# Half of the softmax transposes moved from TensorE to VectorE and a trip through DRAM, with the source's order on every engine

## The chip, the cores and the metric

The kernel runs on one core of a Trainium2 chip. What counts is the time on the device for one execution, in microseconds (us); every time below is in us unless ns is written. Three executions of the kernel before took 957.3, 958.48 and 962.88; the median is 958.48. A further execution was recorded by the hardware profiler, and all rows shown come from it.

## The reference, cut to what matters

One layer of an encoder block, for 512 tokens of width 2048. The normalised input is multiplied by one wide matrix whose columns feed two mixers, attention with 16 heads of 64 and a gated linear attention (GLA) with 4 heads; both results are gated and go through an output matrix.

```python
h = rms_norm(x) * (1.0 + scale[:, None]) + shift[:, None]
proj = h @ w_in[layer]
aq, ak, av, ag, gq, gk, gv, gg, lr_f, lr_b = jnp.split(proj, PROJ_SPLITS, axis=-1)
...
s = jnp.einsum('bnqrhe,bnkrhe->bhrnqk', qb, kw) * (E ** -0.5)   # one of three patterns
s = jnp.where(mask, s + bias[None, :, None, None], NEG_INF)
m = jnp.max(s, axis=-1, keepdims=True)
p = jnp.exp(s - m)
den = jnp.sum(p, axis=-1, keepdims=True)
o = jnp.einsum('bhrnqk,bnkrhe->bhrnqe', (p / den), vw)
...
a_out = att.reshape(B, S, ATT_WIDTH) * jax.nn.silu(ag)
g_out = g_o * jax.nn.silu(gg)
y = jnp.concatenate([a_out, g_out], axis=-1) @ w_out[layer]
return rms_norm(x + gate[:, None] * y) * final_gain
```

The three patterns are merged with weights from their softmax denominators. That is the same as one dense softmax over all 512 keys, with the logarithm of the number of patterns that hold a key added to the bias, and this is what the kernel computes. For each head it needs P, 512 by 512 after the softmax, once with queries on the partitions (for the sums over keys) and once turned, with keys on the partitions (for the product with the values).

## The kernel before, in words

**Units.** The big products are cut into units of 512 output columns: qk2, qk4, qk6 (queries and keys of two pairs of heads each), gk, gv0, gv1 (GLA's keys and values), ag0, ag1, gg0, gg1 (the gates), o0 to o3 (the output matrix). Two earlier stages, sa and sb, make the values and the first queries and keys. A unit has four output tiles, each in a PSUM buffer of its own, `ps_..._0` to `ps_..._3`, and 16 steps along the inner dimension of 2048, two to a fetched weight group. Every product is made of three TensorE matmuls (function `three`, L168 to L171), since numbers are split in a high part and a low rest: high by high, high by low, low by high.

**Weights.** A group of 512 KB is fetched on SyncE's queue (`fetch`, L282 to L286) into one of four RAW buffers, its high part is copied on ScalarE (`split_hi`, L313, 128x1024) and its low part taken by a subtraction on VectorE (`split_lo`, L297, 128x1024), into three buffers each.

**Attention as side work.** While TensorE goes through qk2, qk4, qk6 and gk, the four heads of the two pairs whose queries and keys the unit before made are attended to between its matmuls. A head has four tiles of 128 queries, so each unit has 16. The short names in the prediction are s, p and t with head and tile: s71 is the score of head 7's tile 1, p71 its P, t71 its turned tile. Each tile takes

- `score`: two matmuls (L576, L577) into a PSUM buffer of the "pa" tag (three of them), a pass on VectorE that adds the bias and takes the row's minimum of the negated logits (L580), exp on ScalarE (L583), a reciprocal on VectorE (L584) and a scaling on GpSimd (L585);
- `turn`: four TensorE transposes into a "pa" buffer (L597), a copy of the high part on ScalarE (L601) and the low rest on VectorE (L602), into `pt`, which holds two tiles (a half head);
- `values`, once a half: eight matmuls (L611), a copy on ScalarE (L614) and a sum on VectorE (L618) into `cat`.

A list `items` puts a tile's turn two places after its score and a half's products one after its second turn; `ATT_AT` spreads the list over the unit, and `unit` (L843) issues each item at its tick, 64 ticks to a unit.

**Between units** `qk_evict` (L531) empties the four output tiles: for each head ScalarE makes `qs` and `ks` (L539, L548), VectorE the rest of `qs` and `kl` (L540, L550), and four small transfers on SyncE's queue bring the other half of the partitions (L549, L551). Queries and keys lie in "pj" buffers, of which there are five, so the next unit's second tile needs the first of them emptied.

**Other side work.** The adaLN shift and gate need column sums over matrices that are read once: 48 sums on VectorE, `bias_half` for the values' bias (`rawv`) and `gate_half` (`rawg`, L244), each with a load of 512 KB on SyncE's queue. `SUMS_IN` says how many lie in each unit. The GLA heads lie beside gv1, ag0, ag1 and gg0.

**What sets the order.** TensorE always follows the order in which the source calls its instructions (`tc.manual_schedule(engines={E.PE})`). Up to the end of sb all engines follow a plan made in the kernel. From qk2 on the other engines, GpSimd, VectorE, ScalarE and SyncE (`PLANNED`), get their order from a scheduler that goes by priorities; side work is lifted by

```python
with tc.high_priority(offset=20):
    go()
```

Of the kernel before, what the change touches and what calls it, by code (L numbers as in the profile page):

```python
# [10 lines left out]
F32 = mybir.dt.float32  # L11
F32R = mybir.dt.float32r
# [60 lines left out]
ATT_AT = (0.17, 0.8, 0.04, 0.05, 0.05)  # L73
# [4 lines left out]
SUMS_IN = {"qk6": 4, "gk": 4, "gv0": 9, "gv1": 2, "ag0": 7, "ag1": 9, "gg0": 9}  # L78
# [55 lines left out]
def block_kernel(ctx: ExitStack, tc: tile.TileContext, a: dict):  # L134
# [147 lines left out]
    def fetch(i):  # L282
        if i < len(groups) and i not in raws:
            u, g = groups[i]
            raws[i] = RAW(f"raw_{u}{g}", [2, 512])
            nc.sync.dma_start(raws[i], a["w_" + u][g])  # L286
# [244 lines left out]
    def qk_evict(p, psq, psk):  # L531
# [3 lines left out]
        for j in range(2):  # L535
            own = slice(64 * j, 64 * j + 64)
            oth = slice(64 - 64 * j, 128 - 64 * j)
            qs = T2(f"qs{p}{j}", F32R)
            act(qs[own], psq[own, ::-1], AF.Copy, scale=-0.125)  # L539
            stt(qs[oth], psq[own, ::-1], -0.125, qs[own].bitcast(F32),  # L540
                op0=ALU.mult, op1=ALU.subtract)
            stacks[2 * p + j] = [qs, None, None, own]
        for j in range(2):
            own = slice(64 * j, 64 * j + 64)
            oth = slice(64 - 64 * j, 128 - 64 * j)
            ks = T2(f"ks{p}{j}", F32R)
            kl = T2(f"kl{p}{j}", F32R)
            act(ks[own], psk[own], AF.Copy)  # L548
            nc.sync.dma_start(ks[oth].bitcast(F32), ks[own].bitcast(F32))  # L549
            tt(kl[own], psk[own], ks[own].bitcast(F32), op=ALU.subtract)  # L550
            nc.sync.dma_start(kl[oth].bitcast(F32), kl[own].bitcast(F32))  # L551
            stacks[2 * p + j][1:3] = ks, kl
# [3 lines left out]
    def attention(pairs):  # L556

        tiles = [(2 * p + j, i) for p in pairs for j in range(2) for i in range(4)]
        gt, pt, pr_ = {}, {}, {}
        heads = [2 * p + j for p in pairs for j in range(2)]  # L560

        def g_load(h):
            g = gp.tile([P, 896], F32, tag="g", name=f"g{h}")
            nc.sync.dma_start(g, bass.AP(grow.tensor, grow.offset + h * 1024, [[1, P], [1, 896]]))
            gt[h] = g

        def score(h, i):
            def go():
                if h % 8 == 0 and i == 0:
                    cat[h // 8] = B8(f"cat{h // 8}", [4, 512])  # L570
# [12 lines left out]
                act(t, t, AF.Exp, bias=st[:, 0:1], scale=-1.0, accum_out=st[:, 1:2])  # L583
                nc.vector.reciprocal(st[:, 2:3], st[:, 1:2])  # L584
# [4 lines left out]
        def turn(h, i):  # L589
            def go():  # L590
# [7 lines left out]
                hi = pt[h, half][:, 0, :, P * ii:P * ii + P]  # L598
                lo = pt[h, half][:, 1, :, P * ii:P * ii + P]
# [4 lines left out]

        def values(h, half):
            def go():
                t = pt.pop((h, half))
# [24 lines left out]
        at = [start + (q + 0.5) / len(items) * span for q in range(len(items))]  # L632
        at[0] -= move0
        at[1] -= move1
        at[-1] += move_last
        return list(zip(at, items))
# [206 lines left out]
    def unit(name, natural, side=(), rhs=None, lr=None, tiles=range(4)):  # L843
# [5 lines left out]
        for q in range(KT // 2):  # L849
            g = gorder[q] if name == "o3" else q  # L850
            i0 = gi[name, g]
            todo = []
            if 0 in tiles:
                todo = list(range(gi[name, gorder[0] if name == "o3" else 0], upto[name, g] + 1))
                for i in todo:
                    split_hi(i)
                for ahead in (1, 2):
                    fetch(upto[name, g] + ahead)
            if i0 not in low:
                split_lo(i0)  # L860
            hi, lo = wts[i0]
            for n, i in enumerate(tiles):
                for kk in range(2):
# [267 lines left out]
```

## Time and profile before

| what | value |
|---|---|
| median of three executions | 958.48 |
| the profiled execution, whole | 959.9 |
| its span, first to last instruction | 957.9 |
| TensorE busy (page, share of the span) | 939.7 (98%) |
| VectorE busy | 605.3 (63%) |
| ScalarE busy | 431.5 (45%) |
| GpSimd busy | 81.1 (8%) |
| mean granted clock of TensorE | 0.997 |
| DMA, mean over the span | 171 GB/s |

The page counts an engine as busy while one of its instructions runs; the loads of weights into TensorE (PEld) overlap its matmuls and are counted apart. A busy share is a mean over stages. The views that follow break it down: stretches of the span, the time that an engine waited and for whom, and a timeline in which each instruction has its start, its length and, in brackets, the idle time before it and what ended that. A line number such as L597 is the line of the kernel that issued the instruction.

### The profile page before, as it was taken

What the parts mean: (1) busy time and instruction counts of PE and PEld (TensorE: products, weight loads), DVE (VectorE), ACT (ScalarE), POOL (GpSimd) and SP (SyncE); (2) the same over time, 40 slices, a digit from 0 to 9 for tenths busy, and PEclk for the clock granted to TensorE, in tenths of its full rate; (3) what the DMA queues carried; (4) which work ended last, traced back from release to release, by engine and by line L of the source; (5) the groups of instructions that cost most, each with busy time, mean ns of one, the idle gap of its engine ahead of it and who ended that gap; (6) DMA issues with size and microseconds to landing.
All of it is one profiled execution on the core that took longest, in us unless ns stands there. A gap on an engine that the chain in (4) does not pass through costs nothing.

```text
span 957.9 us, 11999 instructions
## 1 busy us (share of the span) xinstructions
PE 939.7 (98%) x4464; PEld 777.1 (81%) x4464; DVE 605.3 (63%) x900; ACT 431.5 (45%) x719; POOL 81.1 (8%) x100
## 2 busy tenths in 40 slices
PE   8999999999999999999999999999999999999996
PEld 5888788888888888888778888888887888888884
DVE  7988899675756676766435656675964352546421
ACT  5443533565655655655215544543834152233222
POOL 0000000012122022122000000000010000202120
PEclk9999999999999999999999999999999999999998
DMA  9999687443333463533454244354555464244013
GB/s 330 413 411 365 229 296 275 150 131 105 112 103 105 144 200 108 173 127 103 150 176 146 86 132 154 132 176 154 173 195 183 132 221 154 92 151 152 23 55 121
DMA packets 45180, 163.76 MB, mean 171 GB/s; under 512 B 5730, under 2 KB 6018, under 8 KB 40386
## 3 DMA queue, kind: packets, MB, share of 16 engines
q1 hardware_dynamic: 44946, 162.68, 49.9%
q8 instruction: 35, 0.57, 0.2%
q10 hardware_dynamic: 176, 0.33, 0.1%
q14 instruction: 23, 0.18, 0.1%
HBM read 154.51 MB, written 4.28 MB: 166 GB/s over the span
## 4 chain that ended last, share of the span: by engine, by line
PE 84%; DMA 6%; DVE 5%; issue 3%; ACT 1%; SPq 0%; POOL 0%; ACTq 0%; DVEq 0%; POOLq 0%
PE ps_o L170 6%; PE ps_o L169 6%; PE ps_o L171 6%; DMA rawg<-in_wg 6%; PE ps_qk L170 5%; PE ps_qk L169 5%; PE ps_qk L171 5%; PE o L611 3%; PE sta L169 3%; PE sta L170 3%; PE sta L171 3%; PE stb L171 3%; PE stb L169 3%; PE stb L170 3%; PE ps_gv L171 3%; PE ps_gv L170 3%
## 5 line engine op out<-in xcount | busy, mean ns | idle before, releaser
L585 POOL TENSOR_SCALAR p<-p,st 128x512 f32<-128x512 f32 x64 | 45.5, 711 | 406.6 <-DVE st L584 357.9
L244 DVE CUSTOM_DVE_ANT_0 cb<-cb,sb,c_bcond 128x2048 f32<-128x2048 f32 (+1 forms) x32 | 73.4, 2294 | 0.0
L583 ACT ACTIVATE p<-p,st 128x512 f32<-128x512 f32 x64 | 46.1, 721 | 56.8 <-DVE st L580 56.3
L602 DVE TENSOR_TENSOR pt<-t,pt 128x512 fp32r<-128x512 f32 x64 | 44.0, 689 | 16.2 <-ACT pt L601 15.8
L580 DVE CUSTOM_DVE_ANT_0 p<-s,g 128x512 f32<-128x512 f32 x64 | 43.6, 687 | 14.8 <-PE s L577 14.5
L601 ACT ACTIVATE pt<-t 128x512 fp32r<-128x512 f32 x64 | 37.8, 592 | 10.2 <-PE t L597 9.2
L244 DVE CUSTOM_DVE_ANT_0 rawg<-rawg,sb,gate 128x1024 f32<-128x1024 f32 x16 | 20.5, 1283 | 29.6 <-DMA rawg<-in_wg 29.6
L611 PEld LDWEIGHTS o<-pt,vv 128*128 128x128 f32 x256 | 34.7, 188 | 5.0 <-DVE pt L602 2.2
L597 PEld LDWEIGHTS t<-c_ident,p 128*128 128x128 f32 x256 | 31.8, 140 | 8.5
L597 PE MATMUL t<-c_ident,p 128*128 128x128 f32 x256 | 38.3, 272 | 0.0
L611 PE MATMUL o<-pt,vv 128*128 128x256 f32 x256 | 36.6, 283 | 0.9 <-DVE pt L602 0.8
L244 DVE CUSTOM_DVE_ANT_0 rawg<-rawg,sb,c_bcond 128x1024 f32<-128x1024 f32 x16 | 20.5, 1283 | 26.3 <-DMA rawg<-in_wg 26.3
L1014 POOL TENSOR_TENSOR x<-x,fgain 128x512 f32<-128x512 f32 x12 | 20.3, 1696 | 185.3 <-ACT ysq L1012 185.3
L1012 ACT ACTIVATE ysq<-x 128x512 f32<-128x512 f32 x16 | 10.1, 632 | 47.2 <-DVE x L1010 47.2
L767 POOL TENSOR_SCALAR dc<-st,sc 128x256 f32<-128x256 f32 x16 | 10.4, 652 | 245.5 <-DVE st L764 240.6
L1009 DVE TENSOR_TENSOR y<-ps_o,sb 128x512 f32<-128x512 f32 x16 | 10.9, 684 | 25.9 <-PE ps_o L171 25.9
L584 DVE RECIPROCAL st<-st 128x1 f32<-128x1 f32 x64 | 10.3, 162 | 24.9 <-ACT p L583 24.9
L576 PE MATMUL s<-ks,qs 128*128 128x512 f32 x64 | 25.1, 391 | 0.0
L577 PE MATMUL s<-kl,qs 128*128 128x512 f32 x64 | 25.0, 391 | 0.0
L774 ACT ACTIVATE sq<-st,sc 128x256 f32<-128x256 f32 x24 | 12.2, 509 | 26.8 <-DVE st L769 14.3
L1010 DVE TENSOR_TENSOR x<-y,x 128x512 f32<-128x512 f32 x16 | 18.0, 1125 | 0.3
L614 ACT ACTIVATE oh<-o 64x256 f32<-64x256 f32 x32 | 12.2, 382 | 13.0 <-PE o L611 12.2
(1275 smaller groups left out, 2916.7 us busy)
## 6 DMA issues: line engine op xcount, KB each, us to landing
cb<-in_wm SPq DMA_DIRECT2D x31, 1024.0 KB, 7.9
rawg<-in_wg SPq DMA_DIRECT2D x32, 512.0 KB, 3.4
raw_o<-in_w_o SPq DMA_DIRECT2D x32, 512.0 KB, 3.4
raw_qk<-in_w_qk SPq DMA_DIRECT2D x24, 512.0 KB, 3.4
rawb<-in_w_sb SPq DMA_DIRECT2D x16, 512.0 KB, 4.8
rawv<-in_wv SPq DMA_DIRECT2D x16, 512.0 KB, 3.8
raw_gv<-in_w_gv SPq DMA_DIRECT2D x16, 512.0 KB, 3.5
raw_ag<-in_w_ag SPq DMA_DIRECT2D x16, 512.0 KB, 3.3
```

The source lines that it names most:

```text
L169: mm(ps, lh, rh, start=first, stop=False)
L170: mm(ps, ll, rh, start=False, stop=False)
L171: mm(ps, lh, rl, start=False, stop=last)
L244: nc.vector.tensor_tensor_reduce(out=w, in0=w, in1=with_, op0=ALU.mult, op1=ALU.add, scale=1.0, scalar=init, accum_out=dst)
L576: mm(ps, qs[:, q], ks, start=True, stop=False)
L580: nc.vector.tensor_tensor_reduce(out=t, in0=ps, in1=gt[h][:, P * i:P * i + 512], op0=ALU.add, op1=ALU.min, scale=1.0, scalar=3e38, accum_o ...
L583: act(t, t, AF.Exp, bias=st[:, 0:1], scale=-1.0, accum_out=st[:, 1:2])
L585: nc.gpsimd.tensor_scalar(t, t, st[:, 2:3], 1.0, op0=ALU.mult, op1=ALU.mult)
L597: nc.tensor.transpose(pk[:, kt * P:kt * P + P], t[:, kt * P:kt * P + P], ident)
L601: act(hi, src, AF.Copy)
L602: tt(lo, src, hi.bitcast(F32), op=ALU.subtract)
L611: mm(po[:, :256], vv[h // 4][:, kt, h % 4, :], t[:, w, kt, :], start=kt == 0 and w == 0, stop=kt == 3 and w == 1)
```

## The change

P is turned in two ways now. In each of the four units, a tile whose head and half are listed in `BY_DVE` (both halves of the first head, the first half of the second and of the third: eight tiles of 16) is transposed by VectorE, which turns blocks of 32x32 in place; the result is stored to DRAM (`leave`, 256 KB) and a half's two tiles are loaded again in four transfers that put the blocks where they belong (`back`, 128 KB each, into a RAW buffer `pf`). ScalarE then makes the high part and VectorE the low rest of the whole half in one instruction each (`part_hi`, `part_lo`), and the products of this half stand later (`BACK_AT`). The other eight tiles go through TensorE as before (`pe_turn`). The reciprocal and the scaling are an item of their own (`scale`).

The order changes with it. From the start of qk2 to the end of gv0 all engines follow the source's order. In qk4, qk6 and gk the first two weight groups are gone through together, tile by tile, so that the second output tile is begun at the 5th step and not at the 3rd. The weights of qk and gk from the fourth group on, and the bias rows `g`, are fetched on ScalarE's queue. `SUMS_IN` takes eight column sums out of qk6 and gk; they stand in later units. The small `lr` weights are loaded and split within gk, and not after it.

```diff
-ATT_AT = (0.17, 0.8, 0.04, 0.05, 0.05)
+ATT_AT = (0.13, 0.0565)
+BY_DVE = ((0, 0), (0, 1), (1, 0), (2, 0))
+BACK_AT = (2.7, 4.6, 5.0, 6.6)
...
-SUMS_IN = {"qk6": 4, "gk": 4, "gv0": 9, "gv1": 2, "ag0": 7, "ag1": 9, "gg0": 9}
+SUMS_IN = {"gv0": 13, "gv1": 3, "ag0": 8, "ag1": 9, "gg0": 9}
...
-            nc.sync.dma_start(raws[i], a["w_" + u][g])
+            queue = nc.scalar if u[:2] in ("qk", "gk") and i > 2 else nc.sync
+            queue.dma_start(raws[i], a["w_" + u][g])
...
@@ qk_evict
-            qs = T2(f"qs{p}{j}", F32R)
+            qs, ks, kl = [T2(f"{n}{p}{j}", F32R) for n in ("qs", "ks", "kl")]
             act(qs[own], psq[own, ::-1], AF.Copy, scale=-0.125)
+            act(ks[own], psk[own], AF.Copy)
             stt(qs[oth], psq[own, ::-1], -0.125, qs[own].bitcast(F32),
                 op0=ALU.mult, op1=ALU.subtract)
-            stacks[2 * p + j] = [qs, None, None, own]
-        for j in range(2):
...
             tt(kl[own], psk[own], ks[own].bitcast(F32), op=ALU.subtract)
-            nc.sync.dma_start(kl[oth].bitcast(F32), kl[own].bitcast(F32))
-            stacks[2 * p + j][1:3] = ks, kl
+            for t in (ks, kl):
+                nc.sync.dma_start(t[oth].bitcast(F32), t[own].bitcast(F32))
+            stacks[2 * p + j] = [qs, ks, kl, own]
...
@@ attention
-            nc.sync.dma_start(g, bass.AP(grow.tensor, grow.offset + h * 1024, [[1, P], [1, 896]]))
+            nc.scalar.dma_start(g, bass.AP(grow.tensor, grow.offset + h * 1024, [[1, P], [1, 896]]))
...
+        def scale(h, i):
+            def go():
+                t, st = pr_.pop((h, i))
                 nc.vector.reciprocal(st[:, 2:3], st[:, 1:2])
                 nc.gpsimd.tensor_scalar(t, t, st[:, 2:3], 1.0, op0=ALU.mult, op1=ALU.mult)
                 pr_[h, i] = t
...
-        def turn(h, i):
+        def pe_turn(h, i):
...
+        def turn(h, i):
+            def go():
+                t = T2(f"pt{h}{i}")
+                nc.vector.transpose(t.rearrange("p (b k r) -> p k b r", b=4, k=4), pr_.pop((h, i)))
+                pr_[h, i] = t
+        def leave(h, i):
+            def go():
+                half, ii = divmod(i, 2)
+                if ii == 0:
+                    away[h, half] = dp.tile([2, P, 512], F32, tag=f"away{h}{half}", name=f"away{h}{half}")
+                nc.sync.dma_start(away[h, half][ii], pr_.pop((h, i)))
+        def back(h, half):
+            def go():
+                t = away.pop((h, half))
+                f = RAW(f"pf{h}{half}", [8, 128])
+                for b in range(4):
+                    nc.sync.dma_start(f[32 * b:32 * b + 32], bass.AP(
+                        t.tensor, t.offset + P * b, [[512, 32], [32 * 512, 8], [1, P]]))
+                pf[h, half] = f
+        def part_hi(h, half):
+            def go():
+                t = pt[h, half] = B8(f"pt{h}{half}", [2, 4, 256], F32R)
+                src = pf[h, half].rearrange("p b (k r) -> p k b r", k=4)
+                act(t[:, 0].rearrange("p k (b r) -> p k b r", b=8), src, AF.Copy)
+        def part_lo(h, half):
+            def go():
+                src = pf.pop((h, half)).rearrange("p b (k r) -> p k b r", k=4)
+                hi, lo = [pt[h, half][:, e].rearrange("p k (b r) -> p k b r", b=8) for e in range(2)]
+                tt(lo, src, hi.bitcast(F32), op=ALU.subtract)
...
-        for x in range(n + 4):
-            if x < n:
-                items.append(score(*tiles[x]))
-            if 2 <= x <= n + 1:
-                items.append(turn(*tiles[x - 2]))
-            if 3 <= x <= n + 2 and tiles[x - 3][1] % 2 == 1:
-                items.append(values(tiles[x - 3][0], tiles[x - 3][1] // 2))
+        for x in range(n):
+            h, i = tiles[x]
+            items.append((x, score(h, i)))
+            items.append((min(x + 0.75, n - 0.6), scale(h, i)))
+            half, ii = divmod(i, 2)
+            if (x // 4, half) in BY_DVE:
+                items.append((x + 1.1, turn(h, i)))
+                items.append((x + 1.5, leave(h, i)))
+                if ii:
+                    for at, piece in zip(BACK_AT, (back, part_hi, part_lo, values)):
+                        items.append((x + at, piece(h, half)))
+            else:
+                items.append((x + 1.8, pe_turn(h, i)))
+                if ii:
+                    items.append((x + 3.6, values(h, half)))
+        items.sort(key=lambda v: v[0])
...
-        start, span, move0, move1, move_last = ATT_AT
...
-        return list(zip(at, items))
+        start, step = ATT_AT
+        return [(start + step * x, go) for x, go in items]
...
@@ unit
+        steps = [order_[:2]] if name in ("qk4", "qk6", "gk") else [order_[:1], order_[1:2]]
+        for step in steps + [[g] for g in order_[2:]]:
...
+                end = upto[name, step[-1]] + (name[:2] == "qk" and step[-1] == order_[-1])
...
             for n, i in enumerate(tiles):
+                for g in step:
+                    hi, lo = wts[gi[name, g]]
+                    for kk in range(2):
...
+                        if tick == ticks - 4 and name[:2] == "qk":
+                            split_lo(end)
                         while pos < len(side) and side[pos][0] * ticks <= tick:
                             urgent(side[pos][1])
                             pos += 1
...
-    for p in range(2):
-        qk_evict(p, psb["b", 4 + 2 * p], psb["b", 5 + 2 * p])
...
+    with tc.manual_schedule(engines=PLANNED):
+        side = attention((0, 1))
+        for i in range(3):
+            fetch(i)
+        split(0)
+        for p in range(2):
+            qk_evict(p, psb["b", 4 + 2 * p], psb["b", 5 + 2 * p])
+        for n, p in (("qk2", 0), ("qk4", 2), ("qk6", 4)):
+            ps = unit(n, False, side + ([(0.6, shift_row)] if p == 4 else []))
+            side = attention((p + 2, p + 3))
+            for q in range(2):
+                qk_evict(p + 2 + q, ps[2 * q], ps[2 * q + 1])
...
+        ps = unit("gk", False, side + [(0.7, lr_load), (0.85, lambda: lr_part(0)), (0.9, lambda: lr_part(1))])
...
+        ps = unit("gv0", True, some_sums("gv0"), lr=lr_tick)
```

More of the change, by code (lines that the diff above doesn't have):

```diff
@@ L897, in gate_evict @@
         lnexp()
-    for p in range(2):
-        qk_evict(p, psb["b", 4 + 2 * p], psb["b", 5 + 2 * p])
-    for n, p in (("qk2", 0), ("qk4", 2), ("qk6", 4)):
-        ps = unit(n, False, attention((p, p + 1)) + ([(0.05, shift_row)] + some_sums(n) if p == 4 else []))
-        for q in range(2):
-            qk_evict(p + 2 + q, ps[2 * q], ps[2 * q + 1])
-    ps = unit("gk", False, attention((6, 7)) + some_sums("gk"))
-    gla["k"] = B8("gkt", [4, 512])
-    for i in range(4):
-        act(gla["k"][:, i, :], ps[i], AF.Copy)
```

121 lines of the change are left out of this document (63 added, 58 removed).

## The prediction

> **What bounds the kernel now.** I read the busy line of the page first, then the busy time of each engine in stretches, then the list of waits, and only then the timeline. All times are in us.
>
> ```profile
> PE 939.7 (98%) x4464; PEld 777.1 (81%) x4464; DVE 605.3 (63%) x900; ACT 431.5 (45%) x719; POOL 81.1 (8%) x100
> ```
>
> The stretches (columns: length, then busy time and instructions of TensorE, its weight loads, VectorE, ScalarE and GpSimd, granted clock, DMA share, GB/s). The first four lie in qk2, qk4, qk6 and gk, the units with attention beside them, and the last in ag1 and gg0:
>
> ```profile
> 205.00:270.00 65.00, 64.97 (x345) 54.71 (x344) 41.30 (x86) 36.82 (x72) 11.15 (x16) 1.00 0.36 110
> 270.00:336.00 66.00, 65.97 (x352) 55.42 (x352) 41.95 (x88) 37.70 (x73) 10.70 (x16) 1.00 0.38 117
> 336.00:402.00 66.00, 65.97 (x352) 55.53 (x351) 48.09 (x100) 37.34 (x72) 11.03 (x17) 1.00 0.52 163
> 402.00:452.00 50.00, 49.82 (x272) 41.91 (x270) 33.97 (x76) 28.38 (x56) 10.68 (x15) 1.00 0.33 105
> 600.00:727.00 127.00, 124.33 (x628) 104.83 (x627) 89.38 (x125) 62.79 (x103) 6.58 (x8) 1.00 0.53 174
> ```
>
> TensorE has work for 64.97 of 65.00 us and the clock is full, so it alone bounds these units. VectorE works 63% of them and ScalarE 57%. Work taken from TensorE's queue here is won, as long as the others still deliver in time. Today only these waits of TensorE touch the part that is changed:
>
> ```profile
> PE o L611 <- DVE pt L602: 0.8, 1, 0.8
> PE plr L924 <- DVE lrs L917: 0.4, 1, 0.4
> ```
>
> **The change, part by part.** *Transposes off TensorE.* The timeline shows one turn of a tile between projection matmuls:
>
> ```profile
> 203.88 0.39 PE L171 MATMUL ps_qk<-h_lo,qk21h 128*128 128x512 f32 x1
> 204.11 0.60 PE L597 MATMUL t<-c_ident,p 128*128 128x128 f32 x4
> ...
> 204.78 0.40 PE L170 MATMUL ps_qk<-h_hi,qk22l 128*128 128x512 f32 x1
> 205.01 0.40 PE L171 MATMUL ps_qk<-h_lo,qk22h 128*128 128x512 f32 x1
> ```
>
> From L171 to the next L171 it is 1.13; three matmuls at 0.227 (204.78 to 205.01 by the rows) would take 0.68. A turn thus costs 0.45. Eight of a unit's 16 tiles leave TensorE, in four units: 32 x 0.45 = 14.4 won. The two waits above (1.2) also go, since the work behind them is now placed earlier.
>
> *What the other engines get.* Prices:
>
> ```profile
> L583 ACT ACTIVATE p<-p,st 128x512 f32<-128x512 f32 x64 | 46.1, 721 | 56.8 <-DVE st L580 56.3
> L602 DVE TENSOR_TENSOR pt<-t,pt 128x512 fp32r<-128x512 f32 x64 | 44.0, 689 | 16.2 <-ACT pt L601 15.8
> L580 DVE CUSTOM_DVE_ANT_0 p<-s,g 128x512 f32<-128x512 f32 x64 | 43.6, 687 | 14.8 <-PE s L577 14.5
> L601 ACT ACTIVATE pt<-t 128x512 fp32r<-128x512 f32 x64 | 37.8, 592 | 10.2 <-PE t L597 9.2
> L584 DVE RECIPROCAL st<-st 128x1 f32<-128x1 f32 x64 | 10.3, 162 | 24.9 <-ACT p L583 24.9
> L614 ACT ACTIVATE oh<-o 64x256 f32<-64x256 f32 x32 | 12.2, 382 | 13.0 <-PE o L611 12.2 <-ACT p L583 0.4
> L618 DVE TENSOR_TENSOR cat<-o,oh 64x256 f32<-64x256 f32 x32 | 13.3, 416 | 7.3 <-ACT oh L614 6.8
> L540 DVE SCALAR_TENSOR_TENSOR qs<-ps_qk,qs 64x512 fp32r<-64x512 f32 x12 | 8.3, 689 | 0.4
> L550 DVE TENSOR_TENSOR kl<-ps_qk,ks 64x512 fp32r<-64x512 f32 x12 | 8.3, 689 | 0.9 <-ACT ks L548 0.6
> L539 ACT ACTIVATE qs<-ps_qk 64x512 fp32r<-64x512 f32 x12 | 7.1, 591 | 2.3 <-DVE qs L540 2.2
> ```
>
> ```profile
> 204.36 1.06 ACT L313 ACTIVATE qk24h<-raw_qk 128x1024 fp32r<-128x1024 f32 x1 [1.47 <-issue]
> 205.45 1.23 DVE L297 TENSOR_TENSOR qk24l<-raw_qk,qk24h 128x1024 fp32r<-128x1024 f32 x1 [1.13 <-ACT qk24h L313]
> ```
>
> The four `part_hi` and `part_lo` of a unit have the shape of the weight splits, 1.06 and 1.23. They replace eight L601 (0.59) and eight L602 (0.69). The block turn on VectorE is in no row: below it lies the reciprocal (0.16), above it the split of twice the elements (1.23); I take L602's 0.69, the same shape. VectorE then gains 8 x 0.69 + 4 x 1.23 - 8 x 0.69 = 4.9 a unit, about 47 of 62: no bound by throughput. The order decides.
>
> In the Trainium skill, "VectorE: DVE Perf Modes", "The three transpose paths", gives VectorE 311 ns for one 128x128 bf16 turn and only 32x32 blocks, and its rules send full 128x128 turns to TensorE. Four such would be an estimated 1.24 a tile; no run here shows it. The sum would be 4.4 longer by it, as in the third rival.
>
> *The round trip.* Per unit eight stores of 256 KB and sixteen loads of 128 KB join SP's queue; weight fetches of qk and gk, and the bias rows, move to ScalarE's queue, where a wait holds all later activations.
>
> ```profile
> g<-grow SPq DMA_DIRECT2D x16, 448.0 KB, 4.4
> out<-x SPq DMA_DIRECT2D x16, 256.0 KB, 2.6
> ks<-ks SPq DMA_DIRECT2D x16, 128.0 KB, 2.2
> ```
>
> ```profile
> 199.90 0.45 SPq L286 DMA_DIRECT2D raw_qk<-in_w_qk  x1
> ```
>
> A store lands 2.6 after issue. Four loads take 4 x 0.45 to issue and 2.2 to 4.4 to land. In the order, head 4's second tile is scored 12.4 into its unit, is turned by 17.5 and stored by 20.2. The loads queue behind the next tile's store (21.7) and land at 26.2 (28.4 at worst). ScalarE reaches `part_hi` at 27.3, products stand at 31.8. So the trip is hidden by the five steps in between; at its worst it shifts that chain by 1.1, which the slack of the second half does not hold: 0 to 4 in all, I take 2.
>
> *Source's order.* Handoffs, from the timeline: a score's second matmul to the reduction, exp to reciprocal to GpSimd, a turn to its copy, and the eviction's ping-pong, where ScalarE waits for VectorE on one PSUM tile:
>
> ```profile
> 203.20 0.39 PE L577 MATMUL s<-kl,qs 128*128 128x512 f32 x1
> 203.63 0.69 DVE L580 CUSTOM_DVE_ANT_0 p<-s,g 128x512 f32<-128x512 f32 x1 [0.54 <-PE s L577]
> ```
> ```profile
> 208.11 0.72 ACT L583 ACTIVATE p<-p,st 128x512 f32<-128x512 f32 x1 [0.47 <-DVE st L580]
> 208.96 0.16 DVE L584 RECIPROCAL st<-st 128x1 f32<-128x1 f32 x1 [0.28 <-ACT p L583]
> 209.29 0.70 POOL L585 TENSOR_SCALAR p<-p,st 128x512 f32<-128x512 f32 x1 [1.75 <-DVE st L584]
> ```
> ```profile
> 206.40 0.60 PE L597 MATMUL t<-c_ident,p 128*128 128x128 f32 x4
> 207.03 0.60 ACT L601 ACTIVATE pt<-t 128x512 fp32r<-128x512 f32 x1 [0.29 <-PE t L597]
> ```
> ```profile
> 190.65 0.68 DVE L540 SCALAR_TENSOR_TENSOR qs<-stb,qs 64x512 fp32r<-64x512 f32 x1 [1.71 <-ACT qs L539]
> 191.37 0.59 ACT L539 ACTIVATE qs<-stb 64x512 fp32r<-64x512 f32 x1 [0.75 <-DVE qs L540]
> ```
> ```profile
> 210.68 0.94 PE o L611 x8
> ```
>
> Counting the changed order of TensorE from a unit's first matmul (0.227 a matmul, 0.45 a turn, 0.94 a half's products, the last row being from the chain), unit qk4 is 61.9 long, 65.5 before. Its end, by the rows above (V VectorE, A ScalarE):
>
> ```
> TensorE: s71 53.3, t70 55.8, t71 59.7, s73 60.8, end 61.9, ps_qk6_1 66.0, t73 68.4
> V reduce p71 -54.8; A exp p71 -55.6, qk60h -56.6; V qk60l -57.9
> A fetch of qk63 waits for qk60l, part_hi -59.0, copy of t70 -59.6; V low of t70 -60.3
> V part_lo -61.6, reduce p72 -62.3, qk61l, cat, reciprocal, low of t71, reduce p73 -65.5
> A exp p73 -66.3, qs40 -66.9; V qs40, kl40, qs41 -69.1, five more evictions -72.5
> V reciprocal p73 -72.7; GpSimd p73 -73.5
> ```
>
> VectorE stands idle 1.9 for exp and the split's high part, 1.8 for ScalarE's fetch, part and copy, and 1.4 for the last exp and qs40, and everything behind stands with it. TensorE pays: t71 needs the PSUM buffer of t70 (60.4 for 59.7), s73 that of s72 (late 1.5 in all), ps_qk6_1 the buffer that qs41 empties (69.1 for 67.6, late 3.05), and t73 needs GpSimd's scaling, whose reciprocal stands behind all eight evictions (73.5 for 71.4): 5.2 a boundary, three boundaries, 15.6.
>
> In the middle of a unit the same happens in small: the low part of t53 ends at 42.6 (ScalarE does part, copy, exp p60 and split one after another), and s62 wants its buffer at 41.7; then p62 is scaled at 50.3 for t62 at 49.5. Together 1.8, four units, 7.2. From gk to gv0, without q and k to evict, 0.7 for s153 and 0.6 for the copy of gk: 1.3. At the start of qk2 the first score stands at 6.1 as before; its operands (kl00 evicted at 192.0, landing 2.2 later) are hidden by these six us.
>
> *The rest.* The two merged first steps and the earlier weight splits change no count; they hide the eviction up to 4.1 and cost their place in the chain above. Of the column sums, eight leave qk6 and gk; four more stand in gv0, where each load follows its predecessor and VectorE is half idle, one each in gv1 and ag0, two in gg1. The 2.7 idle in 600:727 go with 18 sums, 0.15 each: 0.5.
>
> Sum, from the profiled execution's own 959.9: - 14.4 - 1.2 + 15.6 + 7.2 + 1.3 + 2.0 + 0.5 = 970.9. That execution lies 1.4 above the median of the runs; so 969.5.
>
> **Rivals.** *Only the tail is late.* If VectorE and ScalarE catch up before s73, its reduction ends at 62.2, exp 62.9, qs40 63.5, eight evictions 69.3, GpSimd 70.2 for 68.35: 1.85 a boundary. 959.9 - 15.6 + 5.6 + 0.5 - 1.4 = 949.0, faster by 1.0%. For it: the chain above counts every instruction at its full length and every handoff in full, with nothing overlapped. Against: three of the idle stretches follow from who stands in front of whom, not from lengths.
>
> *Nothing is late* and TensorE stays full: 959.9 - 15.6 - 1.4 = 942.9. For it speaks 37% idle VectorE; against it that p73's reciprocal stands behind eight evictions. That the transposes would stay is excluded: the order has 128 fewer on TensorE.
>
> *The block turn is dear*, 1.23: two of them lie in the middle chain of each unit, 4 x 1.1 = 4.4: 973.9.
>
> *The trip is late.* If loads land at 4.4 and stores as late, every turned half (16) comes 3 to 4 later against 2.3 of slack, `part_hi` holds exp behind it, and TensorE waits about 1.3 each: 2.0 is replaced by 21, 988. For it: g's 4.4 beside weights; against: DMA share 0.36.
>
> **How the numbers follow.** About 1% (948.9 to 968.1) is what a measurement of this kernel tells from no change. The forecast has 0.48; its steps may each be off by some tenths, so it spreads over 960 to 984, three quarters of it over 968.1. The tail alone has 0.20, half on each side of 948.9; nothing late 0.06; dear turn 0.13; late trip 0.13. Slower: 0.36 + 0.12 + 0.12 = 0.60; faster: 0.10 + 0.06 = 0.16; within 0.24. The range 948 to 988 leaves out the full TensorE, half of the first rival's lower side and half of the late trip. The forecast's own range is 960 to 984.
>
> **What would show it.** Right: 128 fewer L597-like transposes and TensorE waits near each unit's end for VectorE's eviction, reduction and GpSimd, 5 us a boundary; units of 68 to 69. Wrong: TensorE at 99% in the units (nothing late), waits of `part_hi` on the loads (trip), or a block turn far from 0.69. A granted clock under 1.00 after a wait would add what no step here holds.

## The result, and the profile after

The changed kernel takes 983.19 (median of four, 980.78 to 984.45) against 957.91 of the kernel before beside it: ratio 1.0249, interval 1.0209 to 1.0289. It is slower by 25, where the forecast had 11 (969.5). The direction was right and the size was not. Of all executions below, one of e16 (1038.94, at a granted clock of 0.85) is in a slow state and is left out of that run's median.

The page's busy line of the changed kernel:

```profile
PE 937.6 (96%) x4336; PEld 766.3 (78%) x4336; DVE 621.8 (63%) x917; ACT 428.1 (44%) x704; POOL 83.0 (8%) x100
```

128 fewer instructions, as forecast, but TensorE's share falls from 98% to 96% and its busy time by 2.1 only: an instruction that starts after a stall is recorded longer (0.50 for 0.39 at 263.18 below), so busy time hides part of a stall. Stretches of the span are the better view. The stretches here go from the first matmul of a unit to the first of the next (columns as in the prediction). Kernel before, units qk4, qk6, gk and gv0:

```profile
257.30:323.70 66.40, 66.37 (x353) 55.90 (x352) 41.93 (x89) 37.43 (x72) 11.17 (x16) 1.00 0.36 108
323.70:390.30 66.60, 66.57 (x355) 55.89 (x354) 47.24 (x100) 37.60 (x73) 11.13 (x16) 1.00 0.51 162
390.30:457.50 67.20, 66.36 (x353) 55.91 (x352) 44.98 (x94) 36.50 (x70) 12.05 (x16) 1.00 0.42 132
457.50:510.40 52.90, 52.52 (x234) 41.21 (x233) 20.16 (x26) 12.16 (x15) 0.00 (x0) 1.00 0.46 150
```

The changed kernel, units qk2, qk4, qk6, gk and gv0:

```profile
192.80:257.60 64.80, 60.50 (x289) 48.99 (x288) 39.92 (x80) 31.39 (x58) 10.74 (x14) 1.00 0.59 176
257.60:329.90 72.30, 65.04 (x321) 52.44 (x320) 45.64 (x92) 36.39 (x69) 12.10 (x16) 1.00 0.53 157
329.90:405.90 76.00, 66.92 (x322) 53.57 (x322) 45.87 (x92) 36.80 (x70) 11.15 (x16) 0.98 0.55 163
405.90:479.20 73.30, 67.40 (x321) 54.65 (x320) 45.44 (x94) 35.99 (x71) 12.19 (x16) 0.95 0.55 162
479.20:535.80 56.60, 55.76 (x258) 43.92 (x257) 30.67 (x46) 17.22 (x25) 1.39 (x2) 1.00 0.59 199
```

The forecast was 68 to 69 for a unit; qk4, qk6 and gk have 72 to 76. VectorE has the same share of work in qk4 as before (63%), ScalarE less, the clock is below full in two units, and the DMA share is up from 0.36 to 0.53 in qk4. Who held TensorE, from the list of its waits (total, times, longest; a few rows left out):

```profile
PE t L602 <- POOL p L589: 9.5, 9, 2.4
PE t L602 <- DVE pt L606: 4.2, 4, 1.5
PE s L573 <- DVE st L577: 3.4, 7, 1.0
PE o L659 <- DVE pt L648: 3.3, 4, 0.9
...
PE ps_qk L173 <- DVE qs L546: 2.4, 2, 1.2
```

**Between two units.** TensorE at the end of qk2 and the start of qk4, then VectorE:

```profile
252.11 1.11 PE L659 MATMUL o<-pt,vv 128*128 128x256 f32 x8
254.72 0.63 PE L602 MATMUL t<-c_ident,p 128*128 128x128 f32 x4 [1.51 <-DVE pt L606]
...
263.18 0.50 PE L173 MATMUL ps_qk<-h_hi,qk40h 128*128 128x512 f32 x1 [1.20 <-DVE qs L546]
...
267.87 0.66 PE L602 MATMUL t<-c_ident,p 128*128 128x128 f32 x4 [2.06 <-POOL p L589]
...
270.45 0.39 PE L573 MATMUL s<-ks,qs 128*128 128x512 f32 x1
```
```profile
261.01 0.68 DVE L546 SCALAR_TENSOR_TENSOR qs<-ps_qk,qs 64x512 fp32r<-64x512 f32 x1 [1.43 <-ACT qs L544]
...
266.04 0.69 DVE L548 TENSOR_TENSOR kl<-ps_qk,ks 64x512 fp32r<-64x512 f32 x1
266.76 0.16 DVE L588 RECIPROCAL st<-st 128x1 f32<-128x1 f32 x1
```

This is what the prediction drew: t31 waits for t30's copy, the second output tile (263.18) for the first eviction, and t33 (267.87) for a scaling whose reciprocal (266.76) stands behind eight evictions. From the products at 252.11 to the first score of the next pair at 270.45 it takes 18.3; the same instructions at the prediction's prices are 12.1. The stall is 6.2, and 5.9 and 6.2 at the next two boundaries (a lower clock there, told below, is not counted in them).

**In the middle of a unit.** Head 4's first half comes back from DRAM in qk4. SyncE's and ScalarE's queues, then the landing times of the four loads (min/median/max, in the view of the tile pf from 283.5 to 286.5), then rows picked from the timelines of ScalarE, VectorE and TensorE:

```profile
283.79 1.85 SPq L632 DMA_DIRECT2D pf<-away  x4
284.16 0.36 ACTq L291 DMA_DIRECT2D raw_qk<-in_w_qk  x1
284.56 0.44 ACTq L563 DMA_DIRECT2D g<-grow  x1
```
```profile
DMA to landing us min/median/max: 2.4/5.4/7.1
```
```profile
291.60 0.39 PE L573 MATMUL s<-ks,qs 128*128 128x512 f32 x1
292.34 1.06 ACT L641 ACTIVATE pt<-pf 128x1024 fp32r<-128x1024 f32 x1 [3.64 <-DMA pf<-away]
293.43 1.23 DVE L648 TENSOR_TENSOR pt<-pf,pt 128x1024 fp32r<-128x1024 f32 x1 [4.54 <-ACT pt L641]
294.71 1.10 PE L659 MATMUL o<-pt,vv 128*128 128x256 f32 x7 [0.87 <-DVE pt L648]
297.23 0.66 PE L602 MATMUL t<-c_ident,p 128*128 128x128 f32 x4 [0.71 <-POOL p L589]
...
318.39 0.60 PE L602 MATMUL t<-c_ident,p 128*128 128x128 f32 x4
```

Within 1.9 us two queues issue four loads of 128 KB, a weight fetch of 512 KB and bias rows of 448 KB. The last load lands 7.1 after its issue. `part_hi` waits for it and holds ScalarE for 3.64, with every exp and copy behind it; VectorE, in its own source order, waits 4.54 for `part_lo`. From s53 at 291.60 to t63 at 318.39 TensorE needs 26.8 for 22.1 of work, a stall of 4.7; it is 4.2, 5.5 and 5.5 in the other units. In the Trainium skill, "DMA: Bandwidth & Descriptors", "Issuing engines are not separate DMA queues", says that transfers issued on several engines save only issuing time. This case agrees as to the loads: on SyncE's queue, the last of them lands after 7.1 beside the two fetches on ScalarE's queue, and after 5.2 in e5 below, where one of the two stands elsewhere.

**The clock.** In the first 20 us of qk6, and TensorE behind the longest stall there:

```profile
329.90:350.00 20.10, 16.48 (x80) 13.30 (x80) 12.66 (x26) 9.98 (x21) 2.08 (x3) 0.92 0.40 109
```
```profile
340.51 0.66 PE L602 MATMUL t<-c_ident,p 128*128 128x128 f32 x4 [2.41 <-POOL p L589]
340.92 0.64 PE L173 MATMUL ps_qk<-h_hi,qk61h 128*128 128x512 f32 x1
341.35 0.63 PE L174 MATMUL ps_qk<-h_hi,qk61l 128*128 128x512 f32 x1
```

Matmuls start 0.43 apart, not 0.23, for 3.4 us: about 1.65 lost at the start of qk6 and of gk each. A third such stretch, from 447.9 to 450.3, lies in the middle of gk; about 1.1 of the 5.5 counted there as a stall is this clock.

### The profile page after: what moved, and what is told of

Read it like the earlier page. It is cut to its first block, busy times and chain, and to the rows that moved or that the text cites. A ratio compares the mean times of both kernels' runs of the same rounds, so it can differ in the third digit from the quotient of the medians.

```text
span 981.5 us, 11837 instructions
## 1 busy us (share of the span) xinstructions
PE 937.6 (96%) x4336; PEld 766.3 (78%) x4336; DVE 621.8 (63%) x917; ACT 428.1 (44%) x704; POOL 83.0 (8%) x100
## 4 chain that ended last, share of the span: by engine, by line
PE 39%; DVE 8%; DMA 8%; issue 5%; ACT 5%; POOL 1%; SPq 0%; ACTq 0%; DVEq 0%; POOLq 0%
PE ps_o L173 6%; PE ps_o L174 6%; PE ps_o L175 6%; DMA rawv<-in_wv 3%; DMA rawg<-in_wg 3%; PE ps_gg L174 2%; PE ps_gg L173 2%; PE ps_gg L175 2%; DMA pf<-away 2%; PE go L858 1%; PE ps_ag L173 1%; PE ps_ag L175 1%; PE ps_ag L174 1%; PE ps_gv L175 1%; PE ps_gv L173 1%
## 5 line engine op out<-in xcount | busy, mean ns | idle before, releaser
L589 POOL TENSOR_SCALAR p<-p,st 128x512 f32<-128x512 f32 x64 | 47.6, 743 | 435.1 <-DVE st L588 339.8
L606 DVE TENSOR_TENSOR pt<-t,pt 128x512 fp32r<-128x512 f32 x32 | 22.0, 687 | 24.2 <-ACT pt L605 23.6
L602 PE MATMUL t<-c_ident,p 128*128 128x128 f32 x128 | 20.9, 288 | 13.8 <-POOL p L589 9.5
L648 DVE TENSOR_TENSOR pt<-pf,pt 128x1024 fp32r<-128x1024 f32 x16 | 20.0, 1249 | 19.7 <-ACT pt L641 19.4
L602 PEld LDWEIGHTS t<-c_ident,p 128*128 128x128 f32 x128 | 15.2, 145 | 20.9 <-POOL p L589 13.4
L573 PE MATMUL s<-ks,qs 128*128 128x512 f32 x64 | 26.9, 421 | 4.8 <-DVE st L577 3.4
L248 DVE CUSTOM_DVE_ANT_0 rawg<-rawg,sb,gate 128x1024 f32<-128x1024 f32 x16 | 20.7, 1293 | 14.5 <-DMA rawg<-in_wg 14.5
L666 DVE TENSOR_TENSOR cat<-o,oh 64x256 f32<-64x256 f32 x32 | 13.2, 413 | 18.2 <-ACT oh L662 17.9
L641 ACT ACTIVATE pt<-pf 128x1024 fp32r<-128x1024 f32 x16 | 16.9, 1054 | 17.9 <-DMA pf<-away 15.3
L614 DVE STREAM_TRANSPOSE pt<-p 128x512 f32<-128x512 f32 x32 | 22.7, 709 | 2.6 <-POOL p L589 2.5
```

The source lines that it names most:

```text
L248: nc.vector.tensor_tensor_reduce(out=w, in0=w, in1=with_, op0=ALU.mult, op1=ALU.add, scale=1.0, scalar=init, accum_out=dst)
L573: mm(ps, qs[:, q], ks, start=True, stop=False)
L589: nc.gpsimd.tensor_scalar(t, t, st[:, 2:3], 1.0, op0=ALU.mult, op1=ALU.mult)
L602: nc.tensor.transpose(pk[:, kt * P:kt * P + P], t[:, kt * P:kt * P + P], ident)
L614: nc.vector.transpose(t.rearrange("p (b k r) -> p k b r", b=4, k=4), pr_.pop((h, i)))
```

## The experiments

Each is an edit of the changed kernel (983.2) unless another is named; "before" is the kernel before, run on the same chip. The lengths of units in us, from the starts of their first matmuls:

| kernel | qk2 | qk4 | qk6 | gk | gv0 | median |
|---|---|---|---|---|---|---|
| before | 65.4 | 66.4 | 66.6 | 67.2 | 52.9 | 958 |
| changed | 64.8 | 72.3 | 76.0 | 73.3 | 56.6 | 983.2 |
| e1, all by TensorE | 63.3 | 71.1 | 71.2 | 69.5 | 54.5 | 970.8 |
| e2, no trip | 61.6 | 69.5 | 71.7 | 68.6 | 56.6 | 966.5 |
| e4, scheduler | 60.2 | 63.5 | 64.2 | 64.3 | 55.1 | 946.5 |
| e5, bias rows later | 63.5 | 70.4 | 76.1 | 71.9 | 56.5 | 976.4 |
| e6, scaling first | 64.9 | 72.1 | 74.3 | 71.8 | 56.5 | 978.7 |
| e19, first halves | 58.5 | 62.4 | 62.6 | 62.8 | 55.0 | 942.0 |

**e1: all tiles by TensorE.**

```diff
-BY_DVE = ((0, 0), (0, 1), (1, 0), (2, 0))
+BY_DVE = ()
```

> All 16 tiles of a unit are turned by TensorE (BY_DVE empty); source's order, fetch queue, merged steps and sums stay as in the changed kernel. Theory A (in the changed kernel the stalls in the middle of a unit, about 5 us each, come from loads of P that land late and hold part_hi and with it ScalarE; the stalls between units, about 6 us each with 1.7 more for the lower clock behind two of them, come from the order): the four stalls in the middle shrink to 0 to 1.8 each, those between units stay, 14.4 of transposes come back: 983.2 - 20 + 14.4 = 971 to 978. Rival B (the order alone makes all stalls): 983.2 + 14.4 - 0 = about 995. Rival C (VectorE's turns and their trip make all stalls, those between units too): 958 to 962.

Measured 970.8, ratio to before 1.0133 (1.0114 to 1.0152). Less work on VectorE and more on TensorE makes the changed kernel faster by 12. TensorE's start times show no stall in the middle of qk4 (5.0 late at s42, 5.6 at s73), and those between units stay. Theory A holds, at the lower end of its range. Without a single turn on VectorE the kernel is still 12 slower than before; the order makes that, for the same kernel in the scheduler's order (e8 below) takes 955.4.

**e2: no trip.**

```diff
...
-                nc.sync.dma_start(away[h, half][ii], pr_.pop((h, i)))
+                away[h, i] = pr_.pop((h, i))
...
-                src = pf[h, half].rearrange("p b (k r) -> p k b r", k=4)
-                act(t[:, 0].rearrange("p k (b r) -> p k b r", b=8), src, AF.Copy)
+                for e, f in enumerate(pf[h, half]):
+                    src = f.rearrange("p (b k r) -> p k b r", b=4, k=4)
+                    act(t[:, 0, :, P * e:P * e + P].rearrange("p k (b r) -> p k b r", b=4), src, AF.Copy)
...
```

> The changed kernel without the trip: no stores, no loads; part_hi and part_lo read the two turned tiles where VectorE left them, in two instructions of 128x512 each, so the 32x32 blocks are not put in their places (this part of the computation is left out). All else and the order stay. Theory A: the stalls in the middle of a unit fall from about 5 us to 1 to 2 each: 983.2 - 12 to - 16 = 967 to 971; those between units stay. Rival B (the order of VectorE and ScalarE makes them): within 3 us of 983.

Measured 966.5, ratio 1.0079 (1.0063 to 1.0095): the trip, with the loads, stores and RAW buffers that it takes, costs the changed kernel 16.7, though VectorE turns as many tiles. From s53 to t63 in qk4 it is 23.3, not 26.8, a stall of 1.1 for 4.7. Theory A holds, with half a us more than its range.

**e5: the bias rows two tiles later.**

```diff
-                if i == 1 and h != heads[-1]:
+                if i == 3 and h != heads[-1]:
```

> The bias rows g of the next head are fetched two tiles later (at i == 3 of a head, not at i == 1), so that 448 KB no longer stand beside the first half's loads of P. Theory A (these loads are late because weights and g are fetched in the same microsecond): their last landing comes about 2 us earlier, as 448 KB at the 207 GB/s of that stretch; the stall in the middle of four units shrinks by 1 to 2 each: 975 to 980. Rival B (the loads are late by themselves or it is the order): 982 to 985. A new wait is possible where g now comes late for the next head's first score: then slower.

Measured 976.4, ratio 1.0188 (1.0151 to 1.0225): 6.8 gained by 448 KB moved to another moment, though its four executions spread from 972.7 to 981.3, so the size is rough. The same four loads in qk4 (view of the tile pf, 281 to 286):

```profile
DMA to landing us min/median/max: 2.4/2.7/5.2
```

`part_hi` now waits 0.7 for them, and the stall in the middle of qk4 falls from 4.7 to 2.7. So much of the lateness is a collision, not the trip's own length: the weight fetch still stands beside these loads, and in the changed kernel the loads issued from 300.2, with no fetch beside them, land within 3.1. What makes up the other 10 of e2's 16.7 was not taken apart.

**e4: the scheduler's order on all engines but TensorE.**

```diff
-    with tc.manual_schedule(engines=PLANNED):
+    with ExitStack():
```

> The changed kernel, but from qk2 to gv0 VectorE, ScalarE, GpSimd and SyncE get their order from the scheduler again; only TensorE keeps the source's order. Theory A: the stalls between units go (18 and about 3 for the clock), since an eviction, an exp or a reciprocal no longer stands behind whatever the source has ahead of it; the late loads stay: 983.2 - 21 = 958 to 966. Rival B (the source's order costs nothing, the engines have too much to do): 980 or more. Rival C (the scheduler hides the late loads too): 945 to 950.

Measured 946.5, ratio 0.9873 (0.9858 to 0.9888): the same instructions, with the same order on TensorE, are 36.7 faster, and faster than before: rival C. All that is left of TensorE's waits for attention:

```profile
PE o L659 <- DVE pt L648: 3.0, 8, 0.7
...
PE s L573 <- DVE pt L606: 0.5, 2, 0.3
```

VectorE between qk2 and qk4 in this kernel:

```profile
254.72 0.68 DVE L548 TENSOR_TENSOR kl<-ps_qk,ks 64x512 fp32r<-64x512 f32 x1
255.33 0.15 DVE L588 RECIPROCAL st<-st 128x1 f32<-128x1 f32 x1
255.50 0.69 DVE L546 SCALAR_TENSOR_TENSOR qs<-ps_qk,qs 64x512 fp32r<-64x512 f32 x1
256.23 0.69 DVE L548 TENSOR_TENSOR kl<-ps_qk,ks 64x512 fp32r<-64x512 f32 x1
257.05 0.69 DVE L606 TENSOR_TENSOR pt<-t,pt 128x512 fp32r<-128x512 f32 x1
```

The reciprocal and the copy of a turn stand among the evictions, not behind them. From the same products to the same score TensorE needs 12.8 here (249.65 to 262.47), a stall of 0.7 against 6.2. The DMA engines are no less busy, and head 4's loads (view of the tile pf, 275.2 to 277.9) land later than in e5:

```profile
253.40:316.90 63.50, 62.91 (x321) 52.88 (x321) 44.93 (x93) 35.89 (x68) 12.05 (x16) 1.00 0.64 179
DMA to landing us min/median/max: 5.6/6.0/6.0
283.43 1.04 ACT L641 ACTIVATE pt<-pf 128x1024 fp32r<-128x1024 f32 x1
```

But `part_hi` starts at 283.43 right behind a weight split and does not wait, so no exp stands behind it. Over the whole kernel `part_hi` waits 0.5 for its loads here, against 15.3 in the changed kernel.

**e8: that version with all tiles by TensorE.**

```diff
-    with tc.manual_schedule(engines=PLANNED):
+    with ExitStack():
-BY_DVE = ((0, 0), (0, 1), (1, 0), (2, 0))
+BY_DVE = ()
```

> The version with the scheduler's order (946.5), but all tiles turned by TensorE: what is left of the change is the fetch queue, the merged first steps, the moved sums and the places of items. Theory A (the transposes alone bring 14.4 less what their trip costs): 946.5 + 11 to 14.4 = 957 to 961, the kernel before. Rival (the merged steps and queues bring the gain): 946 to 952.

Measured 955.4, ratio 0.9972 (0.9962 to 0.9982), 1.6 below theory A's range. The 32 turns are worth 8.9 of the counted 14.4 in this order, and 3 of the gain over before come from the merged steps, the fetch queue, the moved sums and the places of the items together; which of them was not tried. Beside e1 this is the cleanest comparison of the two orders: the same turns on VectorE cost 12.4 in the source's order (983.2 against 970.8) and win 8.9 in the scheduler's.

**e6 and e10: the order between units.** e6 puts the last tile's scaling before the evictions, e10 moves half of the evictions behind the last turn too.

```diff
-            items.append((min(x + 0.75, n - 0.6), scale(h, i)))
+            items.append((min(x + 0.75, n - 0.8), scale(h, i)))
...  (e10, also)
-            for q in range(2):
-                qk_evict(p + 2 + q, ps[2 * q], ps[2 * q + 1])
+            qk_evict(p + 2, ps[0], ps[1])
+            side.append((0.112, lambda p=p, ps=ps: qk_evict(p + 3, ps[2], ps[3])))
```

> The changed kernel with one place moved: the reciprocal and scaling of a unit's last tile (n - 0.6 becomes n - 0.8 in items) come in the unit and so before the eight evictions on VectorE, not behind them. Theory A (as the prediction had it, t73 waits since the reciprocal of p73 stands behind the evictions): the 2.3 to 2.6 us before t33, t73 and t113 go, the wait of ps_..._1 for the eviction (1.5) stays or grows by 0.2: 983.2 - 7 = 976, or 971 if the two stretches of half clock at the start of a unit (1.65 each) go with it. Rival (VectorE has as much to do there in either order, and the wait moves to the second output tile): 981 to 985.

> As e6_scale_first, in the source's order, and the evictions of the second pair's q and k come as a side item at 0.112 of the next unit, behind t33, t73 and t113 and their copies, not in one block of eight with the first pair's. Theory A (after e6 t33 waits for the sum into cat, which stands behind all eight evictions): the 1.7 us before t33, t73 and t113 go: 978.7 - 5 = 973 to 974; ps_..._1 still waits 1.5 for the first eviction. Rival (the work only moves, and the next score or the fourth output tile waits instead): 977 to 980.

e6 measured 978.7, ratio 1.021 (1.0194 to 1.0226), between theory A and its rival: part of the wait only moved, as the rival has it. GpSimd is no longer what t33 waits for; the next thing behind the evictions is, the sum that frees its PSUM buffer:

```profile
266.30 0.63 PE L602 MATMUL t<-c_ident,p 128*128 128x128 f32 x4 [1.54 <-DVE cat L666]
```

In the profiled execution (979.15) the stretches of half clock are gone (0.997 over the span). The other three took as long (978.05 to 979.44) at clocks of 0.991 to 0.995, so what the clock has of the 4.5 gained is open. e10 measured 973.7, ratio 1.0159 (1.0141 to 1.0178), as theory A had it.

**e13: e10 and the bias rows later.** (Both edits above.)

> As e10_split_evict, and the bias rows fetched two tiles later as in e5_g_later. If the stalls between units and those in the middle are separate causes, the savings add: e10's time less the 6.8 that e5 saved: 966 to 968. If they share a cause (the same VectorE backlog), it stays above 970.

Measured 969.6, ratio 1.0117 (1.01 to 1.0134), between the two theories. The bias rows save 4.1 here for 6.8 alone; with the spread of e5 that does not tell whether the savings add in full or in part. Mending the two places leaves the source's order 23 above the scheduler's.

**e14, e15, e16: which engine's order.**

```diff
-    with tc.manual_schedule(engines=PLANNED):
+    with tc.manual_schedule(engines=PLANNED - {E.DVE}):                 (e14)
+    with tc.manual_schedule(engines=PLANNED - {E.Activation}):          (e15)
+    with tc.manual_schedule(engines=PLANNED - {E.DVE, E.Activation}):   (e16)
```

> The changed kernel; only VectorE's order from qk2 to gv0 is left to the scheduler, ScalarE, GpSimd and SyncE keep the source's. Theory A (the chain goes through both: VectorE idles for ScalarE's copies and exps, and ScalarE's order holds part_hi ahead of exp): freeing VectorE alone mends the reciprocal behind the evictions and little in the middle: 968 to 976. Rival B (VectorE's order is the cause): 946 to 955. Rival C (ScalarE's order is): 980 or more.

> The changed kernel; only ScalarE's order (with the transfers that it issues) is left to the scheduler. Theory A: exp no longer stands behind a part_hi that waits for its loads, the middle mends, the stalls between units stay: 965 to 973. Rival B (VectorE's order): 980 or more. Rival C (ScalarE's): 946 to 955.

> VectorE and ScalarE from the scheduler, SyncE and GpSimd in the source's order. Theory A (it is the two engines' order, not the queues'): within 3 us of the fully scheduled version: 944 to 950. Rival (the source's order of stores and loads on SyncE is part of it): 953 or more.

e14 956.3 (ratio 0.9989, 0.9977 to 1.0), e15 966.1 (1.0092, 1.0069 to 1.0114), e16 953.7 (0.9959, 0.9945 to 0.9974). Freeing VectorE alone wins 26.9 of 36.7, ScalarE alone 17.1, both 29.5. e14 misses theory A and ends just above rival B; e15 is as theory A had it. VectorE's order carries most of the loss: in e14 `part_hi` on ScalarE waits 26.0 for its loads, more than the 15.3 of the changed kernel, and yet most of the time is back. The two gains overlap by 14.5 (26.9 + 17.1 - 29.5); that a wait passes from one engine's queue to the other's, as at 292.34 and 293.43 above, would do that, but is argued here, not shown. The last 7 appear only when SyncE and GpSimd are freed too, so theory A of e16 falls and its rival's range holds; which of these two engines it is was not tried.

**e7, e11, e9, e12, e17, e19: how far the turns carry, in the scheduler's order (946.5).**

```diff
-                if i == 1 and h != heads[-1]:                       (e7)
+                if i == 3 and h != heads[-1]:
-BACK_AT = (2.7, 4.6, 5.0, 6.6)                                      (e11, e12)
+BACK_AT = (2.7, 4.6, 5.0, 7.1)
+BY_DVE = ((0, 0), (0, 1), (1, 0), (1, 1), (2, 0), (2, 1))           (e9)
+BY_DVE = ((0, 0), (0, 1), (1, 0), (1, 1), (2, 0))                   (e12)
+BY_DVE = ((0, 0), (1, 0), (2, 0))                                   (e17)
+BY_DVE = ((0, 0), (1, 0), (2, 0), (3, 0))                           (e19)
```

> The version with the scheduler's order (946.5), and the bias rows two tiles later. Theory A (with that order too the products of a half wait for part_lo because the loads land late): the waits of o for pt, 3.0 in eight, fall to under 1 and the time by 2 to 4: 942 to 945. Rival (the scheduler already hides them, what is left is the splits' own order): 946 to 947.

> The scheduler's version (946.5) with a turned half's products half a place later (6.6 becomes 7.1 in BACK_AT), 1.6 us. Theory A (what is left there is the products' wait for part_lo, 0.55 and 0.62 at two places of a unit, 1.2 x 4): 942 to 945. Rival (a later product keeps its PSUM and B8 buffers longer, or other work takes the wait): 946 to 949.

> The version with the scheduler's order (946.5) with 12 of 16 tiles turned by VectorE (both halves of the first three heads). Theory A (each turn taken from TensorE is worth 0.45 as long as the order lets others keep up): 16 more turns, 946.5 - 7 = 939 to 942. Rival (the RAW buffers that hold the returned tiles, and the trips, which now follow each other, make TensorE or the weight fetches wait): 945 to 955.

> As e11_sched_values_later, with ten turned tiles of 16 (the second half of the second head too). Theory A (12 tiles failed because products waited for part_lo, 13.3 in 17, and this place gives room): 3.6 less than e11, 939 to 942. Rival (a second half in a row finds the RAW buffers and the loads taken, as with 12 tiles): 946 to 956.

> The scheduler's version (946.5) with 6 turned tiles of 16, the second half of the first head through TensorE too. If every turn is worth its 0.45: 8 turns back, 946.5 + 3.6 = 950. If the second half's trip costs more than it brings (the waits of o for pt): 943 to 946.

> The scheduler's version with the first halves of all four heads turned by VectorE, eight tiles of 16. If two halves in a row were the cost in the middle of a unit: 945.1 - 3.6 = 941 to 943. If the last head's trip collides with the evictions and the next unit's first steps: 946 to 955.

| run | turned by VectorE | median | ratio to before |
|---|---|---|---|
| e7 | 8 | 947.1 | 0.9884 (0.9871 to 0.9898) |
| e11 | 8, products later | 956.7 | 0.9984 (0.9973 to 0.9995) |
| e12 | 10, products later | 958.1 | 1.0005 (0.999 to 1.0019) |
| e9 | 12 | 964.2 | 1.0054 (1.0041 to 1.0067) |
| e17 | 6 | 945.1 | 0.9868 (0.9851 to 0.9884) |
| e19 | 8, first halves | 942.0 | 0.9826 (0.9803 to 0.985) |

e7 shows no gain, but it did not move the collision. The scheduler issues the bias rows in qk4 1.37 before the first load in both kernels, e4 and then e7:

```profile
273.90 0.33 ACTq L563 DMA_DIRECT2D g<-grow  x1
275.27 2.72 SPq L632 DMA_DIRECT2D pf<-away  x4
```
```profile
272.76 0.33 ACTq L563 DMA_DIRECT2D g<-grow  x1
274.13 2.43 SPq L632 DMA_DIRECT2D pf<-away  x4
```

The last load lands after 6.0 and 6.2, so e7 tests neither of its theories; that the scheduler's order covers late loads rests on e4. e9 misses theory A by over 20, and its rival's range by 9: with three heads in a row the products wait for their parts,

```profile
PE o L659 <- DVE pt L648: 13.3, 17, 1.5
PE o L659 <- ACT pt L641: 4.2, 4, 1.2
```

while the first halves of all heads (e19) leave no wait of TensorE for attention in the list. e19 is the best version, 16 faster than before. It has as many turns as e4 (946.5) and is 4.5 faster: two halves of one head in a row cost what single ones don't. The 1.4 by which e17 is faster than e4 lies within the intervals. e11 came out as neither of its theories: half a place later for the products made it 10 slower. e12, with the same place and ten turns, lies above both of its ranges too. TensorE in e11's qk6:

```profile
362.24 1.09 PE L602 MATMUL t<-c_ident,p 128*128 128x128 f32 x4 [3.54 <-DVE pt L606]
```

VectorE's timeline has a weight split and a `part_lo` (1.23 and 1.22) ahead of the copy that frees this turn's buffer. Why the scheduler chose so there is open; the time of this kernel hangs on such choices by 10 us.

## Why the prediction was wrong, step by step

- **The transposes, -14.4.** Right as to TensorE's work. Where nothing stalls, its start times agree with the count: s40 at 270.45 to s53 at 291.60 is 21.15 for a counted 21.1.
- **What the other engines get.** Right, by the rows of the changed kernel below. A block turn takes 0.709 where 0.69 was taken, and VectorE works 45.6 in qk4 where about 47 was counted. The 1.24 estimated from "VectorE: DVE Perf Modes" in the Trainium skill does not hold for this one instruction of 128x512 in 32x32 blocks; the dear turn falls as a rival.

```profile
L614 DVE STREAM_TRANSPOSE pt<-p 128x512 f32<-128x512 f32 x32 | 22.7, 709 | 2.6 <-POOL p L589 2.5
L648 DVE TENSOR_TENSOR pt<-pf,pt 128x1024 fp32r<-128x1024 f32 x16 | 20.0, 1249 | 19.7 <-ACT pt L641 19.4
L641 ACT ACTIVATE pt<-pf 128x1024 fp32r<-128x1024 f32 x16 | 16.9, 1054 | 17.9 <-DMA pf<-away 15.3
```

- **Between units, 15.6.** Right in mechanism (t71, the second output tile, t73 behind the eight evictions), 18.3 measured. From gk to gv0 (1.3) two waits of 0.40 and 0.44, for the copy of gk and for a sum, cost 1.2 by the start times.
- **The clock** was in no term: 1.65 at the start of qk6 and gk each, 3.3.
- **The middle of a unit, 7.2, and the trip, 2.0.** This is the step that failed. "So the trip is hidden by the five steps in between" rested on loads that land after 2.2 to 4.4; the last load of each unit's first half lands after 6.7 (qk2), 7.1, 7.5 and 7.6 (gk). The prediction counted how many transfers join SyncE's queue, and not that fetches on ScalarE's queue share the same engines in the same microsecond. Measured 19.9 (4.2, 4.7, 5.5, 5.5) for 9.2. e2 puts it on the trip, e5 in part on its collision, and e4, where `part_hi` waits 0.5 in all, shows that it costs so much only in the source's order. The rival "the trip is late" had this mechanism, but not in the forecast, and with all 16 halves late; here `part_hi` waits for its loads in four, 15.3 in all (row L641 above).
- **The old waits, 1.2.** As a term too small: qk4, qk6 and gk of before lie 3.4 above their counted 65.5, 65.8 and 65.5. But only 0.8 of it is a wait in the list. TensorE is busy for 66.37 of 66.40 in qk4, so most of the rest is work that the count priced too low, by about 1%; which instructions was not found.
- **The sums, +0.5.** Wrong sign: gv1 to gg0 take 218.5 for 220.3. The start of qk2 comes 0.9 later, which no term held.

From qk2 to gv0 that is -14.4 - 3.4 + 18.3 + 19.9 + 3.3 = 23.7, for 24.5 in the trace, where the step from gk to gv0 is not in the sum; with + 0.9 and - 1.8 outside, the span's 23.6. The forecast's sum had 11.0 in its place. The middle with the trip is 10.7 of the 12.6 between them, the clock 3.3 and the boundaries 2.7; the old waits and the sums went the other way, by 2.2 and 2.3.

## What to carry to other kernels

Work taken off the bounding engine is won only if the queues behind it keep their slack: here turns counted at 14.4 became a loss of 12.4 in a fixed order and a gain of 8.9 in a flexible one. In a fixed order, look for the instruction that waits for a transfer at the head of an engine's queue, and price its transfer with everything that any queue issues in the same microsecond. Space the trips (first halves of four heads) rather than follow one with another.

## What the runs showed of the hardware that was not expected

- A stall can have an echo: after waits of TensorE no longer than 2.41, the granted clock was halved (0.53 to 0.58 over these stretches, their edges included) for 3.4 us and matmuls went 0.43 apart for 0.23. "TensorE: Matmul & The Clock Gate" in the Trainium skill, under "Why this matters for your kernels", asks for no gaps over about 3 us; here it fell with a gap of 2.41 (and 1.2, five us before) at the start of qk6. At the start of gk it fell after 1.2 and 2.07; at the start of qk4 it stayed full after 1.20 and 2.06. In e5 it fell at 398 after a single wait of 1.97, and in e6, with none over 1.54 there, it stayed full. The condition is not settled by these runs.
- A wait of TensorE costs more than its idle time in the list: at 254.72 the list has 1.51, and the start times show 1.67 (2.61 from the products at 252.11, less their 0.94).
- Four loads of 128 KB each land within 3.1 where nothing else is issued beside them (issued from 300.2 in the changed kernel), and within 7.1 beside 960 KB of fetches (issued from 283.8).
